# A decoder layer on one core: the sample's products with cached keys in three pinned steps

## The chip, the core and the metric

The kernel runs on one core of a Trainium2 chip. The core has five engines that run their own instruction streams: TensorE (PE, matmuls; its weight loads are listed apart as PEld), VectorE (DVE), ScalarE (ACT), GpSimd (POOL) and SyncE (SP), which here issues all transfers. [...] The metric is the time of one execution in microseconds on the device: before the change 1337.19 us, the median of three runs (1336.5 to 1340.72).

## The reference

One layer of a hybrid decoder, for a prompt of 2048 tokens and a sample of 8 batches with 8 new tokens each. After an RMS norm, one input projection gives queries, keys and values for 8 heads of 64 (mixer A), the inputs of a gated linear attention (mixer B) and two gates. Mixer A is attention over three dilated windows:

```python
DILATED = ((128, 1), (512, 4), (2048, 16))

def attend_prompt(q, k, v):
    return dilated_mixture([dilated_branch_prompt(qf, kf, vf, w, d) for w, d in DILATED])

def attend_sample(k_past, v_past, q, k, v):
    k_buf = jnp.concatenate([k_past, k], axis=1)
    v_buf = jnp.concatenate([v_past, v], axis=1)
    return dilated_mixture([dilated_branch_sample(qf, k_buf, v_buf, w, d) for w, d in DILATED])
```

For the sample, each of the 64 new tokens (batch b, step t) needs the products of its query with some of the 2048 cached keys of its batch: the last 128, every fourth of the last 512, and every sixteenth of all. What is computed here is the scores `s = einsum('bthd,btnhd->bthn', q, keys) * hd ** -0.5` for dilations 4 and 16. A token's keys for dilation 16 are its own (128 rows of stride 16 from row t); for dilation 4, tokens t and t + 4 share 128 rows.

## The kernel before, in words

**Stages.** (1) Up to about 440 us the prompt is projected to v, q and k, four tiles of 128 tokens at a time (`first(m)`, m = 0 to 3), while the attention of dilations 1 and 4 over the tiles projected earlier is fed in between (`pump`). (2) Then the projection `qkb` runs with the rest of that attention and the one of dilation 16 (`branch3`, whose queries and keys are brought by transposing loads `T_q`, `T_k`). (3) From about 740 us the projections `g`, `vb` and `gb` run beside the gated linear attention (`gla_prompt`) and its sample part. (4) From about 1090 us the output projection (`Y`, L1652) runs beside the sample's softmax and values (`sample_pair`).

**Attention of one unit** (`attend`): TensorE makes scores `s` (L444), VectorE masks and finds the maximum (`p`, L452), ScalarE takes exponentials (L455), TensorE transposes (`t`, L462), and the transposed weights are split into a high and a low half of 16 bits each (`split`). Every other split makes the low half on VectorE (L425, after ScalarE's L424), every other one on GpSimd (L429, after ScalarE's L427 and L428). Then TensorE multiplies with the values (`O`, L477), and ScalarE and VectorE bring the result out (L493, L494).

**Products with cached keys.** For a token t of batch b, `sample_keys` loads the query repeated on 128 partitions (`qb`, L981), the keys of dilation 16 (`k3`, L983) and, for t below 4, those of dilation 4 (`k2`, L986), each 128 x 512 in two buffers. `sample_scores` calls `dot` twice: GpSimd multiplies keys and query into `pr` (L965), which has one buffer, and VectorE sums each 64 of it (L970). After the eighth token a batch's 128 scores are stored (L976). `scores_of` makes a list of 49 steps of this for batches 0 to 5: step i loads token i and multiplies and sums token i - 1. Tokens are taken in the order 0, 4, 1, 5, 2, 6, 3, 7. From m = 2 one step is taken after each projected tile (24 in all), the others are woven into the `qkb` stage (`dots`). For batches 6 and 7, in stage 3, a loop of its own (`late_dots`) does it in three steps, with four buffers of `pr` and products at L1509, and with each step's instructions queued behind the last decay (L236) on GpSimd and the last `qbd` (L252) on VectorE.

**What sets the order.** The program text is written in woven order, but a scheduler places each engine's instructions: among those whose inputs and buffers it holds to be ready by its own estimate of time, the one written first. So an instruction whose inputs are there early can come to stand ahead of others that were written before it. `tc.issue_after(ins)` keeps all instructions of its block that run on the engine of `ins` behind `ins`; it makes no wait on the chip, it only fixes a place in the engine's order. Each engine runs its list strictly in that order, SyncE's transfers too, so one that waits holds all behind it.

## Time and profile before

| what | value |
|---|---|
| median of the runs (three) | 1337.19 us |
| the profiled execution | 1341.12 us, span from first to last instruction 1339.3 us |
| granted TensorE clock, mean | 0.977 |
| busy: PE, PEld | 1215.7 us (91%), 726.8 us (54%) |
| busy: DVE, ACT, POOL | 924.8 us (69%), 876.6 us (65%), 635.4 us (47%) |
| transfers | 285.27 MB, mean 213 GB/s |

In the lines of the profile, `L965 POOL TENSOR_TENSOR pr<-k,qb x96` is line 965 of the kernel before, on GpSimd, with output and inputs by the program's names and the count. "Idle before, releaser" is time in which an engine stood before an instruction, and the instruction or transfer that ended it. A busy TensorE is one with a matmul in its pipeline; that pipeline isn't always at its peak.

### The profile page before, as it was taken

How to read it: one execution, taken by the hardware profiler on the slowest of the kernel's cores; microseconds unless marked ns; L12 is line 12 of the kernel's file. 1: busy time of each engine (PE TensorE's matmuls, PEld its weight loads, DVE VectorE, ACT ScalarE, POOL GpSimd, SP SyncE). 2: the span in 40 equal slices, each digit the busy share in tenths (PEclk: the TensorE clock that was granted, in tenths of full speed). 3: DMA queues.
4: the chain of work that ended last, by engine and by line, in shares of the span. 5: the costliest groups of instructions: out<-in, count | busy, mean ns of one | idle time of the engine just before them, and what ended most of it. 6: DMA issues, size and time to landing. Idle time of an engine off the chain costs nothing.

```text
span 1339.3 us, 26206 instructions
## 1 busy us (share of the span) xinstructions
PE 1215.7 (91%) x8878; PEld 726.8 (54%) x8878; DVE 924.8 (69%) x2275; ACT 876.6 (65%) x2332; POOL 635.4 (47%) x598
## 2 busy tenths in 40 slices
PE   3798999888899798998989899999999979999998
PEld 1343565555566555576667566676554434444443
DVE  6367767788677966776755988777682288778751
ACT  5655787777568875878986666666773366554630
POOL 0076554778678735661113975666362133232220
PEclk9998999999999999999999999999999989999999
DMA  8859856767966599969986556553236679998952
GB/s 256 248 159 254 234 174 155 208 204 216 222 180 192 174 265 281 317 208 212 214 186 184 171 179 200 163 156 119 88 126 192 193 229 342 358 380 293 320 191 79
DMA packets 251800, 285.27 MB, mean 213 GB/s; under 512 B 125441, under 2 KB 160338, under 8 KB 251666
## 3 DMA queue, kind: packets, MB, share of 16 engines
q1 hardware_dynamic: 251666, 283.60, 70.9%
q8 instruction: 70, 1.15, 0.4%
q14 instruction: 64, 0.52, 0.1%
HBM read 183.12 MB, written 75.24 MB: 193 GB/s over the span
## 4 chain that ended last, share of the span: by engine, by line
PE 38%; DVE 18%; DMA 16%; POOL 9%; issue 9%; ACT 8%; SPq 2%; POOLq 0%; DVEq 0%; ACTq 0%
PE Y L1652 4%; PE acc_qkb L1127 3%; PE acc_vb L1127 3%; PE acc_v L1127 3%; PE acc_g L1127 3%; PE acc_gb L1127 3%; PE O L477 3%; PE t L462 3%; PE s L444 3%; DVE qbd L252 3%; PE acc_q L1127 2%; DMA T_q<-qp_d 2%; POOL pr L965 2%; PE acc_k L1127 2%; DMA sv<-in_cache_v_win 2%
## 5 line engine op out<-in xcount | busy, mean ns | idle before, releaser
L1127 PEld LDWEIGHTS <-hr 128*128 128x128 f16 x1824 | 174.5, 99 | 134.3 <-issue 17.4
L1127 PEld LDWEIGHTS <-hl 128*128 128x128 f16 x1248 | 122.1, 100 | 151.8 <-issue 24.3
L455 ACT ACTIVATE p<-p,o 128x256 f32<-128x256 f32 (+1 forms) x384 | 173.3, 456 | 46.4 <-DVE o L452 39.4
L1652 PE MATMUL Y<-w_o,mh 128*128 128x512 f16 x768 | 176.7, 381 | 1.8 <-ACT mh L1611 1.8
L965 POOL TENSOR_TENSOR pr<-k,qb 128x512 f32<-128x512 f32 x96 | 132.5, 1381 | 91.2 <-DVE sck L970 57.1
L429 POOL TENSOR_TENSOR pt<-p,pt 128x512 f16<-128x512 f32 (+1 forms) x80 | 94.2, 1178 | 158.4 <-ACT pt L428 142.6
L477 PE MATMUL O<-v,pt 128*128 128x128 f16 x1200 | 111.4, 222 | 25.5 <-POOL pt L429 9.2
L1652 PEld LDWEIGHTS <-mh 128*128 128x128 f16 x768 | 72.0, 98 | 88.6 <-issue 6.3
L970 DVE TENSOR_REDUCE sck<-pr 128x8 f32<-128x512 f32 x128 | 85.6, 678 | 49.0 <-POOL pr L965 48.8
L462 PE MATMUL t<-ident,p 128*128 128x128 f32 x600 | 107.5, 284 | 8.1 <-ACT p L455 3.5
L1694 POOL TENSOR_TENSOR tc<-oc,w 128x512 f32<-128x512 f32 x32 | 45.2, 1432 | 141.9 <-DVE w L1686 119.1
L477 PEld LDWEIGHTS <-pt 128*128 128x128 f16 x1200 | 82.5, 99 | 51.2 <-POOL pt L429 14.1
L1127 PE MATMUL acc_v<-w_v,hl 128*128 128x512 f16 x384 | 96.4, 396 | 8.1 <-DMA hl<-early_ht 4.0
L1127 PE MATMUL acc_g<-w_g,hr 128*128 128x272 f16 (+1 forms) x768 | 102.6, 279 | 0.0
L452 DVE CUSTOM_DVE_ANT_0 p<-s,m3w,scl_s 128x128 f32<-128x128 f32 (+1 forms) x256 | 88.9, 394 | 11.6 <-PE s L444 6.2
L1127 PE MATMUL acc_q<-w_q,hl 128*128 128x512 f16 x384 | 91.6, 387 | 3.5 <-ACT zs_k L677 2.2
L244 ACT ACTIVATE E<-D_e 128x256 f32<-128x256 f32 x168 | 66.3, 417 | 43.5 <-POOL D_e L236 25.6
L1127 PE MATMUL acc_vb<-w_vb,hr 128*128 128x512 f16 x384 | 92.3, 389 | 2.4 <-ACT zg L733 2.4
L1127 PE MATMUL acc_k<-w_k,hl 128*128 128x512 f16 x384 | 89.9, 379 | 3.4 <-ACT zs_k L677 3.0
L444 PE MATMUL s<-kk,qq 128*128 128x256 f16 (+1 forms) x512 | 82.4, 272 | 9.7 <-DMA kk<-kp_d 6.1
L1127 PE MATMUL acc_gb<-w_gb,hr 128*128 128x512 f16 x384 | 87.1, 380 | 0.0
L462 PEld LDWEIGHTS t<-ident,p 128*128 128x128 f32 x600 | 69.4, 145 | 18.1 <-ACT p L455 8.1
(510 smaller groups left out, 2637.4 us busy)
## 6 DMA issues: line engine op xcount, KB each, us to landing
k<-in_cache_k_win SPq DMA_DIRECT2D x104, 256.0 KB
sv<-in_cache_v_win SPq DMA_DIRECT2D x24, 1024.0 KB
hr<-h_d SPq DMA_DIRECT2D x44, 512.0 KB
qb<-q_d SPq DMA_DIRECT2D x64, 256.0 KB
o_d<-o SPq DMA_DIRECT2D x96, 132.0 KB
oc<-o_d SPq DMA_DIRECT2D x48, 264.0 KB
x<-in_x_prompt SPq DMA_DIRECT2D x16, 512.0 KB
h_d<-hl SPq DMA_DIRECT2D x16, 512.0 KB
```

Of the source, the lines that this page charges most:

```text
L244: ACT.activation(ev[rows, i], dv[rows, :, half, :], AF.Exp, scale=(2 * half - 1) / 16.0)
L429: POOL.tensor_tensor(l, f, h, ALU.subtract)
L444: PE.matmul(s_ps[:, i * w : (i + 1) * w], q, k, start=(n == 0), stop=(n == len(prods) - 1),)
L452: DVE.tensor_tensor_reduce(s[:, sl], s_ps[:, sl], mask, neg, BIG, ALU.add, ALU.min, nmf(i))
L455: ACT.activation(s[:, sl], s[:, sl], AF.Exp, bias=nmf(i), scale=-1.0, accum_out=denf(i))
L462: PE.transpose(p_ps[:, i * P : (i + 1) * P], t["s"][:, i * P : (i + 1) * P], ident[:])
L477: PE.matmul(o_, t["pt"][:, c, (i * nb + b) * P : (i * nb + b + 1) * P], vf(i, b), start=(n == 0), stop=(n == 2 * nb - 1),)
L965: POOL.tensor_tensor(pr[:], kt, qt, ALU.mult)
L970: DVE.tensor_reduce(out, pr[:].rearrange("p (u k d) -> p u k d", u=2, k=4), AX.X, ALU.add)
L1127: PE.matmul(z, a_[:, k, :], w[:, p_, k, cols], start=(k == 0 and i == 0), stop=(k == KT - 1 and i == 2),)
L1652: PE.matmul(Y[:], a_[:, k, :], w_[:, part, k, :512], start=(i == 0), stop=(i == len(prods) - 1),)
L1694: eng.tensor_tensor(t_[:], oc[:, g, :, 0:64], w[:, g].unsqueeze(2).to_broadcast([P, NH, HD]), ALU.mult,)
```

## The change

`scores_of` now has 50 steps and works in three: step i loads token i, multiplies token i - 1 (`products`) and sums token i - 2. Products are written over the keys, except those of `k2` for t below 4, which are needed again for token t + 4 and go to `pr`. The key tile of dilation 16 gets a third buffer. Each step's instructions are placed behind the latest split's low half on GpSimd and on VectorE (`pins`). Batches 6 and 7 use the same code, with the pins at decay and `qbd` as before. The temporary `t1` of the q and k stage is taken from another pool, one that is given back after that stage. The number of products, sums and loads stays.

```diff
--- before.py
+++ after.py
@@ -253,7 +253,8 @@
                 qbd[:, :, :n].rearrange("p i (m B) -> p i m B", B=B),
                 qv[:, :, 1, :].unsqueeze(1).to_broadcast([P, 2, M, B]), ev[:, 1:3], ALU.mult,
             )
-            st["pins"] = (dec.ins, que.ins)
+            pins["POOL"], pins["DVE"] = dec.ins, que.ins
+            gla_on.append(li)
 
         def back(self, li):
             st, n, C, nch, B = self.st, self.n, self.C, self.nch, self.levels[li]
@@ -422,11 +423,13 @@
             h, l = out
             if split_[0] % 2:
                 ACT.activation(h, in_, AF.Copy, scale=P_SCALE)
-                DVE.scalar_tensor_tensor(l, in_, P_SCALE, h, ALU.mult, ALU.subtract)
+                pins["DVE"] = DVE.scalar_tensor_tensor(
+                    l, in_, P_SCALE, h, ALU.mult, ALU.subtract
+                ).ins
             else:
                 ACT.activation(f, in_, AF.Copy, scale=P_SCALE)
                 ACT.activation(h, f, AF.Copy)
-                POOL.tensor_tensor(l, f, h, ALU.subtract)
+                pins["POOL"] = POOL.tensor_tensor(l, f, h, ALU.subtract).ins
 
         def attend(tag, nh, nb, scores, mask, vf, nmf, denf, OT, pre=None, post=None, neg=-1.0):
 
@@ -694,7 +697,7 @@
                 ct[:n, :, :g], cs[:n].unsqueeze(2).to_broadcast([n, 2, g, 64]),
                 tabs[:n, :, i0 : i0 + g], ALU.mult,
             )
-            t1 = zp.tile([P, 2, 512], F32, name=f"t1_{tag}", tag="z3", bufs=1)
+            t1 = xp.tile([P, 2, 512], F32, name=f"t1_{tag}", tag="z3", bufs=1)
             t2 = zp.tile([P, 2, 512], F32, name=f"t2_{tag}", tag="z4", bufs=1)
             z4 = zs[:n, :g].rearrange("p g (h two d) -> p g h two d", two=2, d=32)
             t24 = t2[:n, :g].rearrange("p g (h two d) -> p g h two d", two=2, d=32)
@@ -959,12 +962,6 @@
         q_s = q_d[S : S + NS, :]
         sk_state = {"pool": sk}
 
-        def dot(out, kt, qt, tag):
-            sk = sk_state["pool"]
-            pr = sk.tile([P, 512], F32, name=f"pr_{tag}", tag="pr", bufs=1)
-            POOL.tensor_tensor(pr[:], kt, qt, ALU.mult)
-            sum_of(out, pr)
-
         def sum_of(out, pr):
 
             DVE.tensor_reduce(
@@ -979,35 +976,45 @@
             sk = sk_state["pool"]
             qt = sk_state["q", t] = sk.tile([P, 512], F32, name=f"qb_{b}_{t}", tag="qbc")
             SP.dma_start(qt[:], q_s[8 * b + t : 8 * b + t + 1, :].to_broadcast([P, 512]))
-            k3 = sk_state["k3", t] = sk.tile([P, 512], F32, name=f"k3_{b}_{t}", tag="k3")
+            k3 = sk_state["k3", t] = sk.tile([P, 512], F32, name=f"k3_{b}_{t}", tag="k3", bufs=3)
             SP.dma_start(k3[:], ck[b].rearrange("(m r) c -> r m c", r=16)[t])
             if t < 4:
                 k2 = sk_state["k2", t] = sk.tile([P, 512], F32, name=f"k2_{b}_{t}", tag="k2")
                 SP.dma_start(k2[:], ck[b, W - 512 : W, :].rearrange("(j r) c -> r j c", r=4)[t])
 
-        def sample_scores(b, t):
-            if t == 0:
-                sk_state["sc"] = sk_state["pool"].tile(
-                    [P, 2, 64], F32, name=f"sck_{b}", tag="sc"
-                )
-            sc = sk_state["sc"]
-            out = sc[:].rearrange("p g (u t k) -> p g t u k", u=2, t=8)[:, :, t]
-            qt = sk_state["q", t]
-            dot(out[:, 1], sk_state["k3", t][:], qt[:], f"3_{b}_{t}")
-            dot(out[:, 0], sk_state["k2", t % 4][:], qt[:], f"2_{b}_{t}")
-            if t == 7:
-                keep_scores(b, sc)
+        pins = {}
 
         def scores_of(batches):
             todo = [(b, t) for b in batches for t in (0, 4, 1, 5, 2, 6, 3, 7)]
+            scs, sums = [], []
+
+            def products(b, t):
+                sk = sk_state["pool"]
+                if t == 0:
+                    scs.append(sk.tile([P, 2, 64], F32, name=f"sck_{b}", tag="sc"))
+                out = scs[-1][:].rearrange("p g (u t k) -> p g t u k", u=2, t=8)[:, :, t]
+                for g, k_ in ((1, sk_state["k3", t]), (0, sk_state["k2", t % 4])):
+                    pr = k_
+                    if g == 0 and t < 4:
+                        pr = sk.tile([P, 512], F32, name=f"pr_{b}_{t}", tag="pr", bufs=1)
+                    POOL.tensor_tensor(pr[:], k_[:], sk_state["q", t][:], ALU.mult)
+                    sums.append((out[:, g], pr))
 
             def step(i):
-                if i < len(todo):
-                    sample_keys(*todo[i])
-                if i:
-                    sample_scores(*todo[i - 1])
-
-            return [lambda i=i: step(i) for i in range(len(todo) + 1)]
+                with ExitStack() as order:
+                    for p_ in pins.values():
+                        order.enter_context(tc.issue_after(p_))
+                    for out, pr in sums:
+                        sum_of(out, pr)
+                    sums.clear()
+                    if i > 1 and todo[i - 2][1] == 7:
+                        keep_scores(todo[i - 2][0], scs.pop(0))
+                    if i < len(todo):
+                        sample_keys(*todo[i])
+                    if 0 < i <= len(todo):
+                        products(*todo[i - 1])
+
+            return [lambda i=i: step(i) for i in range(len(todo) + 2)]
 
         nwa = kp.tile([P, KT], F32, name="nwa")
         ACT.activation(nwa[:], nw[:], AF.Abs)
@@ -1255,7 +1262,7 @@
         full = gst.tile([P, 8, P], F32, name="full")
         POOL.memset(full[:], 0.0)
 
-        mixed = set()
+        mixed, gla_on = set(), []
 
         ob_ss = kp.tile([P, 4 * (NT + 1)], F32, name="ob_ss")
         POOL.memset(ob_ss[:], 1.0)
@@ -1476,38 +1483,13 @@
         def late_dots():
             for _ in range(6):
                 yield
-            scs = []
             sk_state["pool"] = c_sk.enter_context(
                 tc.tile_pool(name="sk3", bufs=2, reuse_waits="tile")
             )
-            todo = [(b, t) for b in range(6, 8) for t in (0, 4, 1, 5, 2, 6, 3, 7)]
-            prods, sums = [], []
-            for i in range(len(todo) + 2):
-                while "pins" not in st:
-                    yield WAIT
-                with ExitStack() as order:
-                    for p_ in st["pins"]:
-                        order.enter_context(tc.issue_after(p_))
-                    for out, pr in sums:
-                        sum_of(out, pr)
-                    if i > 1 and todo[i - 2][1] == 7:
-                        keep_scores(todo[i - 2][0], scs.pop(0))
-                    if i < len(todo):
-                        sample_keys(*todo[i])
-                    sums = []
-                    if 0 < i <= len(todo):
-                        b, t = todo[i - 1]
-                        if t == 0:
-                            scs.append(sk_state["pool"].tile(
-                                [P, 2, 64], F32, name=f"sck_{b}", tag="sc"
-                            ))
-                        out = scs[-1][:].rearrange("p g (u t k) -> p g t u k", u=2, t=8)[:, :, t]
-                        for g, k_ in ((1, sk_state["k3", t]), (0, sk_state["k2", t % 4])):
-                            pr = sk_state["pool"].tile(
-                                [P, 512], F32, name=f"pr{g}_{b}_{t}", tag="pr", bufs=4
-                            )
-                            POOL.tensor_tensor(pr[:], k_[:], sk_state["q", t][:], ALU.mult)
-                            sums.append((out[:, g], pr))
+            while not gla_on:
+                yield WAIT
+            for f in scores_of(range(6, 8)):
+                f()
                 yield
             c_sk.close()
             mixed.add("dots")
```

In the order of GpSimd, first quarter of the m = 2 stage, batch 0's tokens 5, 2, 6, 3 (a `pr` in the first, `k` or `pr` in the second, is the output of a product; `pt` is a low half, `t_qk`, `ra_qk`, `qr_qk`, `rv_qk`, `ct_qk` belong to the norm and rotation of q and k). Before:

```order
L429 TENSOR_TENSOR pt_1_0_2_1_3071<-p_1_0_2_1_2930,pt_1_0_2_1_3071 128x512
L135 TENSOR_SCALAR ra_qk_3400<-ra_qk_3400 128x16
L136 TENSOR_TENSOR qr_qk_3397<-ra_qk_3400,rr_qk_3399 128x16
L965 TENSOR_TENSOR pr_0_2_3438<-k_0_2_3293,qb_2_3291 128x512
L429 TENSOR_TENSOR pt_1_0_3_1_3160<-p_1_0_3_1_3079,pt_1_0_3_1_3160 128x512
L965 TENSOR_TENSOR pr_0_2_3441<-k_0_2_3295,qb_2_3291 128x512
L965 TENSOR_TENSOR pr_0_6_3570<-k_0_6_3436,qb_6_3434 128x512
L429 TENSOR_TENSOR pt_1_0_0_1_3258<-p_1_0_0_1_3165,pt_1_0_0_1_3258 128x512
L965 TENSOR_TENSOR pr_0_6_3573<-k_0_2_3295,qb_6_3434 128x512
L965 TENSOR_TENSOR pr_0_3_3693<-k_0_3_3566,qb_3_3564 128x512
L965 TENSOR_TENSOR pr_0_3_3696<-k_0_3_3568,qb_3_3564 128x512
```

And now:

```order
L432 TENSOR_TENSOR pt_1_0_0_1_3252<-p_1_0_0_1_3160,pt_1_0_0_1_3252 128x512
L1000 TENSOR_TENSOR k_0_5_3167<-k_0_5_3167,qb_5_3165 128x512
L1000 TENSOR_TENSOR k_0_1_3028<-k_0_1_3028,qb_5_3165 128x512
L432 TENSOR_TENSOR pt_1_0_1_1_3350<-p_1_0_1_1_3257,pt_1_0_1_1_3350 128x512
L1000 TENSOR_TENSOR k_0_2_3289<-k_0_2_3289,qb_2_3287 128x512
L1000 TENSOR_TENSOR pr_2_3433<-k_0_2_3291,qb_2_3287 128x512
L704 TENSOR_TENSOR t_qk_3796<-zs_q_3659,ct_qk_3794 128x1024
L710 TENSOR_TENSOR t_qk_3797<-zs_q_3659,ct_qk_3794 128x16x32 x2
L122 TENSOR_SCALAR rv_qk_3784<-qs_q_3660 128x16
L432 TENSOR_TENSOR pt_1_0_2_1_3494<-p_1_0_2_1_3358,pt_1_0_2_1_3494 128x512
L1000 TENSOR_TENSOR k_0_6_3430<-k_0_6_3430,qb_6_3428 128x512
L1000 TENSOR_TENSOR k_0_2_3291<-k_0_2_3291,qb_6_3428 128x512
```

Each pair of products now stands behind a low half (L429, now L432), with the next one behind the pair; before, products stood singly or in threes between other work.

In the order of VectorE about the same place, the sums (L970, now L967). Before:

```order
L970 TENSOR_REDUCE sck_2885<-pr_0_5_3300 128x2x4
L425 SCALAR_TENSOR_TENSOR pt_1_0_3_0_3111<-t_1_0_3_0_3106,pt_1_0_3_0_3111 128x512
L713 TENSOR_TENSOR t_qk_3411<-t_qk_3410,qr_qk_3397 128x1024
L759 SCALAR_TENSOR_TENSOR vp_3554<-acc_v_3463,vp_3554 128x8x64
L452 ISA p_1_0_0_1_3165,o_1_0_0_3093<-s_1_0_0_1_3164,m3w,scl_s 128x256
L452 ISA o_1_0_0_3093 128x1
```

And now:

```order
L542 SCALAR_TENSOR_TENSOR ht_3840<-x_2547,rs_3830,ht_3840 128x1024
L426 SCALAR_TENSOR_TENSOR pt_1_0_3_0_3536<-t_1_0_3_0_3531,pt_1_0_3_0_3536 128x512
L967 TENSOR_REDUCE sck_2885<-k_0_2_3289 128x2x4
L967 TENSOR_REDUCE sck_2885<-pr_2_3433 128x2x4
L455 ISA p_1_1_0_1_3601,o_1_1_0_3518<-s_1_1_0_1_3600,m3c,scl_s 128x256
L455 ISA o_1_1_0_3518 128x1
```

The two sums of a token now stand side by side behind a split (L425, now L426), later than the split after which their products stand on GpSimd; before, each stood by itself where its product was estimated to end.

In the order of SyncE, at the third `T_q` of the dilation 16 branch. Before:

```order
L874 DMA o_d<-o_3_1_0_7261 128x264
L155 DMA zqk_e_9831<-zqk_d 128x2x512
L155 DMA zqk_e_10052<-zqk_d 128x2x512
L976 DMA sc_d<-sck_7617 128x128
L874 DMA o_d<-o_3_1_1_7354 128x264
L909 DMA_TRANSPOSE T_q_7756<-qp_d 128x8x128
L909 DMA_TRANSPOSE T_k_7758<-kp_d 128x8x128
L874 DMA o_d<-o_3_1_2_7452 128x264
L730 DMA zqk_d<-zq_8451 128x512
L567 DMA hr_8483<-h_d 128x2048
L909 DMA_TRANSPOSE T_q_7870<-qp_d 128x8x128
```

And now:

```order
L912 DMA_TRANSPOSE T_q_7691<-qp_d 128x8x128
L912 DMA_TRANSPOSE T_k_7693<-kp_d 128x8x128
L877 DMA o_d<-o_3_1_2_7392 128x264
L980 DMA k_5_2_7828<-in_cache_k_win 128x512
L983 DMA k_5_2_7830<-in_cache_k_win 128x512
L570 DMA hr_9462<-h_d 128x2048
L733 DMA zqk_d<-zq_8765 128x512
L978 DMA qb_2_7826<-q_d 128x512
L912 DMA_TRANSPOSE T_q_7804<-qp_d 128x8x128
L912 DMA_TRANSPOSE T_k_7806<-kp_d 128x8x128
L877 DMA o_d<-o_3_1_3_7486 128x264
L980 DMA k_5_6_7941<-in_cache_k_win 128x512
```

Before, all loads of keys and queries for batches 0 to 5 stand ahead of this place. Now those of the last tokens of batch 5 stand among the transposing loads.

## The prediction

> **What bounds the kernel now.** First the stretches of the span. Columns after the length: busy us (instructions) of TensorE matmuls, weight loads, VectorE, ScalarE, GpSimd, then granted TensorE clock, DMA share, GB/s.
>
> ```profile
> 120.00:240.00 120.00, 116.89 (x778) 67.36 (x777) 81.79 (x224) 89.04 (x262) 59.04 (x68) 0.99 0.74 195
> ...
> 240.00:480.00 240.00, 210.76 (x1506) 133.81 (x1505) 193.06 (x473) 178.32 (x499) 181.88 (x162) 0.97 0.74 208
> 480.00:600.00 120.00, 113.10 (x847) 73.45 (x845) 81.43 (x228) 90.62 (x258) 67.28 (x54) 0.99 0.91 260
> ...
> 600.00:740.00 140.00, 128.25 (x1162) 97.19 (x1160) 88.62 (x367) 113.72 (x403) 28.86 (x29) 0.95 0.82 201
> 740.00:930.00 190.00, 180.20 (x1614) 124.60 (x1613) 156.08 (x231) 120.50 (x325) 133.09 (x108) 0.98 0.52 163
> ...
> 1080.00:1100.00 20.00, 10.80 (x57) 5.60 (x56) 16.57 (x40) 11.96 (x21) 12.06 (x10) 0.74 0.66 196
> ```
>
> TensorE sets the pace nearly everywhere, so time can only be won where it stands still. From 120 to 240 us, with projections and prompt attention but no cached keys, it is idle 3.1 of 120 us (2.6%). From 240 to 480, the same two kinds of work with the products over cached keys woven in, it is idle 240 - 210.76 = 29.2 us (12%). From 480 to 600 it is 6.9 us, with DMA at 0.91. GpSimd goes from 49% busy to 76%.
>
> Next, who waits for whom around the products: what the product's engine and the sum's engine sat idle for (us, times).
>
> ```profile
> L965 POOL TENSOR_TENSOR pr<-k,qb x96: 1261/1272/2259, 240.5 to 595.5; 128x512 f32<-128x512 f32 x96
> ...
>   DVE sck L970: 57.1, 42
> ...
> L970 DVE TENSOR_REDUCE sck<-pr x128: 666/678/687, 241.8 to 925.1; 128x8 f32<-128x512 f32 x128
> ...
>   POOL pr L965: 48.8, 38
> ```
>
> GpSimd stood 57.1 us before a product because the one buffer `pr` still waited for its sum on VectorE; VectorE stood 48.8 us before a sum because its product wasn't done. The two engines hold each other in turn, and all that is queued behind is held too. Third, what this does to TensorE between 240 and 600 us (us in total, times, longest), with three waits of the chain in front of it:
>
> ```profile
> PE O L477 <- POOL pt L429: 8.3, 12, 1.4
> PE s L444 <- DMA kk<-kp_d: 6.1, 2, 4.6
> PE t L462 <- ACT p L455: 3.5, 5, 1.5
> PE s L444 <- DVE o L452: 3.5, 5, 2.2
> PE O L477 <- DMA v<-vp_d: 3.3, 2, 2.0
> PE O L477 <- ACT pt L428: 2.9, 2, 2.3
> PE O L477 <- DVE o L494: 2.3, 1, 2.3
> ...
> ACT p L455 <- DVE o L452: 33.7, 25, 4.5
> POOL pt L429 <- ACT pt L428: 22.2, 17, 5.6
> ```
>
> The largest is the value product (L477) waiting for the low half of the weights, which GpSimd makes (L429), the instruction that stands between products. VectorE's masks (L452) are late for ScalarE's exponentials (33.7 us, 25 times), and through L455, L452 and L494 for TensorE (9.3 us). One instance in order of time, first GpSimd, then VectorE:
>
> ```profile
> 378.11 2.19 POOL L965 TENSOR_TENSOR pr<-k,qb 128x512 f32<-128x512 f32 x1 [3.42 <-DVE sck L970]
> 381.09 1.27 POOL L965 TENSOR_TENSOR pr<-k,qb 128x512 f32<-128x512 f32 x1 [0.80 <-DVE sck L970]
> 382.77 1.17 POOL L429 TENSOR_TENSOR pt<-p,pt 128x512 f16<-128x512 f32 x1 [0.41 <-ACT pt L428]
> ...
> 375.92 1.39 DVE L818 COPY qq<-qq 64x2048 f16<-64x2048 f16 x2 [2.45 <-DMA qq<-qp_d]
> 377.35 0.69 DVE L970 TENSOR_REDUCE sck<-pr 128x8 f32<-128x512 f32 x1
> 377.95 1.22 DVE L713 TENSOR_TENSOR t_qk<-t_qk,qr_qk 128x1024 f32<-128x1024 f32 x1
> ```
>
> The sum stood on VectorE behind a copy that waited 2.45 us for a transfer; GpSimd waited 3.42 us for that sum. A late transfer for one attention block thus became a stop of an engine that had nothing to do with it.
>
> **The change part by part.** The sum: profiled execution 1341.12 us (span 1339.3 and 1.8 around it), which is 3.9 above the median 1337.19 of the runs. I work out a difference and apply it to the median.
>
> *(a) Sums a step behind their products, products in place, both pinned behind the latest split.* Same instructions: 96 products of 1.38 us on average and 96 sums of 0.68 us, none added. Their order moves. A product no longer needs the sum ahead of it, since its result lies in the key tile, or in a `pr` that was read a step before; by the order shown above the prediction a sum stands some two splits behind its product. The pins do not make an engine wait at run time; they keep a product from standing ahead of an earlier split. Upper end: the stretch 240 to 480 falls to the idle share of 120 to 240, 0.026 x 240 = 6.2 us, so 29.2 - 6.2 = 23.0 us are won. Lower end: nothing. In between lies the list of waits. What the mutual stop can account for is L429's 8.3 us and the 9.3 us behind VectorE, 17.6 in all; the rest is late transfers and ScalarE. L429 also waited 22.2 us for ScalarE, as in the last GpSimd row above, and that stays. I take 60% of 23.0, which is 13.8, near three quarters of the 17.6. From 480 to 600 the excess is 6.9 - 3.1 = 3.8 us, but DMA is nearly full there: I take 1.
>
> *(b) The third key buffer.* A key tile is now held through its sum, so loads would come a step later with two buffers. SyncE's own waits from 240 to 600 us:
>
> ```profile
> SPq L983 <- POOL pr L965: 33.0, 18, 5.2
> SPq L981 <- POOL pr L965: 27.2, 23, 4.4
> ```
>
> SyncE stood 60.2 us before loads of keys and queries whose buffer a product held, with transposes of `kk` and `qq` and loads of `v` queued behind. With GpSimd freed, these buffers come free sooner; the k3 loads have a spare one. The two-buffer k2 tiles and the queries have none. This is how the 9.4 us of TensorE waiting for `kk` and `v` could shrink; it is inside (a)'s upper end, and I add nothing. The query loads' wait does not depend on the sums.
>
> *(c) Two steps more of delay, one step more in number.* The last products move past the end of dilation 4's attention. GpSimd's order has no product behind the last L429 of that branch before, and 12 now; with them go 12 sums and the loads of some 5 steps, about 12 transfers of 256 KB, 3 MB. They fall into the stretch from 600 us, which is bound by other loads:
>
> ```profile
> DVE T_q L818 <- DMA T_q<-qp_d: 26.6, 11, 3.4
> ```
>
> The work of 12 x 1.38 = 16.6 us on GpSimd (busy 28.86 of 140) and 12 x 0.68 = 8.2 us on VectorE (88.62 of 140) has cover. If it stood uncovered on VectorE it would cost 8.2 us. The transfers have little: 3 MB at 201 GB/s is 15 us of DMA time at a share of 0.82, but the same bytes leave the stretch before. Between 0 and 8 us, I take 3, since only some of those loads stand directly ahead of a `T_q`.
>
> *(d) Batches 6 and 7, 740 to 930 us.* Already in three steps and pinned; what changes is in-place products instead of four `pr` buffers. SyncE's waits there:
>
> ```profile
> SPq L983 <- POOL pr L1509: 14.4, 10, 3.0
> ...
> SPq L981 <- POOL pr L1509: 7.5, 10, 1.3
> ```
>
> Smaller than before by far, with DMA at 0.52. A key tile is held for a sum longer, and k3 has a tile more: 0, between -2 and +2.
>
> *(e) The tile t1 in another pool.* No instruction changes, but the room that later pools get does. In the last stage the sample's memsets and first loads stand earlier, ahead of TensorE's first output transposes:
>
> ```profile
> 1092.30 1.04 PE L1610 MATMUL tm<-ident,mt 128*128 128x128 f16 x8 [8.86 <-ACT mt L1600]
> ...
> 1088.22 0.42 SPq L1762 DMA_DIRECT2D hm<-in_c_hm  x1
> ...
> 1092.02 0.45 SPq L1778 DMA_DIRECT2D ls_q<-q_d  x1
> ```
>
> TensorE stands 8.86 us there. Sample transposes (L1781, L1807, L1830) can fill up to some 3 us of that if their loads land in time; if these land late, the first transpose of the output waits behind them. Between -3 and +3; I take -1, because the loads now stand ahead of three `oc` loads.
>
> Sum: -13.8 - 1 + 0 + 3 + 0 - 1 = -12.8 us, so 1324.4; I say 1325. All lower ends: -23.0 - 3.8 - 2 - 3 = -31.8, 1305. All upper ends: +8 + 2 + 3 = +13, 1350.
>
> [...] Products have a minimum of 1.261 us, but a mean of 1.381:
>
> ```profile
> L965 POOL TENSOR_TENSOR pr<-k,qb 128x512 f32<-128x512 f32 x96 | 132.5, 1381 | 91.2 <-DVE sck L970 57.1 <-DMA qb<-q_d 9.9 <-PE O L477 6.3
> ```
>
> The one at 378.11 took 2.19 us while VectorE ran L713 until 379.17; 379.17 + 1.27 is 380.44, its end was 380.30. So it ran after L713, not beside it. [...] Excess so far: 96 x (1.381 - 1.272) = 10.5 us. [...]
>
> **The rivals.** A measurement of this kernel tells a change from none at about 0.3%, 4 us.
>
> *More is won.* TensorE's idle share falls all the way to that of 120 to 240, `kk` and `v` come in time too: -23 - 2 + 3 - 1 = -23, 1314. For it: the 60.2 us of SyncE's waits; against: DMA at 0.74 is no less in 120 to 240, but the 22.2 us that GpSimd waits for ScalarE stay.
>
> [...]
>
> *Another wait takes the place.* TensorE's next limits are ScalarE (22.2 us for L428) and transfers. If L429 comes no earlier because ScalarE or the step's two back-to-back products (2.8 us) hold it, only some 5 us are won and 3 given back: 1335, no change.
>
> *Slower: the loads of late steps among those of dilation 16.* SyncE issues in order. Between the `T_q` transposes now stand some 12 loads of keys and queries, each of which can wait for a buffer that a pinned product or sum on a busy engine holds. At the mean of the waits above, 60.2/41 = 1.5 us, they hold the queue 18 us, in a stretch where `T_q` is already what is late (26.6 us). If two thirds of that reach TensorE, 12 us, and (a) yields 6: 1337.2 + 6 = 1343. It decides once (a) yields less than what the held `T_q` cost. Against: GpSimd is only 21% busy there, so buffers come free at once.
>
> **How the numbers follow.** The forecast (1318 to 1331) 0.41; more won 0.18; ports 0.10; another wait 0.17; slower 0.14. Forecast and more won are faster by over 0.3%, and so are two thirds of the ports' case: 0.66. Same: 0.17 + 0.03 = 0.20. Slower: 0.14. The likeliest's own range is 1318 to 1331; to leave out 2 in 10, half of the slower case and the far end of more won, the range is 1309 to 1341.
>
> **What would show it.** Right: GpSimd's idle time before products put down to L970 nearly gone (from 57.1), VectorE's before sums under 10 (from 48.8); TensorE idle between 240 and 480 us near 15 instead of 29; its wait for L429 below 4 us; the end of the dilation 4 branch some 13 us earlier. (c) right: products after 600 us with TensorE's idle share from there to the end of dilation 16 little changed. [...] Wrong altogether: TensorE's idle time as before with ScalarE or DMA as what ended it, or the gain up to 600 us gone by 740.

## The result, and the profile after

The changed kernel takes 1346.03 us (median of four runs, 1345.03 to 1346.35). Beside it the kernel before took 1337.19 us (median of three runs of 1336.5 to 1340.72; a fourth, disturbed one of 2480 us is left out). The ratio is 1.0058, 95% interval 1.0035 to 1.0080: **slower** by 0.6%, where 1325 us had been predicted with a range up to 1341. The same two kernels run again (e13 below) give 1.0053 (1.0035 to 1.0071). The profiled execution of the changed kernel took 1345.03 us (span 1343.2, mean granted clock 0.973).

To see where the time went, TensorE's own work serves as a ruler, since both kernels have the same matmuls. The view of a source line gives for each kind of matmul the count, the duration in ns (min/median/max), and when the first and the last of them started. Kernel before: projections of k, the last three quarters of qkb, gb; scores of dilation 16; output products.

```profile
L1127 PE MATMUL acc_k<-w_k,hl x384: 376/379/379, 83.8 to 441.7; 128*128 128x512 f16 x192
L1127 PE MATMUL acc_gb<-w_gb,hr x384: 379/379/390, 954.5 to 1083.1; 128*128 128x512 f16 x192
L1127 PE MATMUL acc_qkb<-w_qkb,hr x288: 379/379/631, 501.3 to 617.9; 128*128 128x512 f16 x144
...
L1652 PE MATMUL Y<-w_o,mh x768: 379/379/634, 1094.5 to 1334.5; 128*128 128x512 f16 x192
...
L444 PE MATMUL s<-T_k,T_q x256: 216/219/314, 599.5 to 713.2; 128*128 128x128 f16 x128
```

The same view of the changed kernel:

```profile
L1134 PE MATMUL acc_k<-w_k,hl x384: 377/380/380, 88.1 to 432.2; 128*128 128x512 f16 x192
L1134 PE MATMUL acc_gb<-w_gb,hr x384: 378/380/391, 954.8 to 1081.5; 128*128 128x512 f16 x192
L1134 PE MATMUL acc_qkb<-w_qkb,hr x288: 378/380/391, 489.5 to 597.4; 128*128 128x512 f16 x144
...
L1634 PE MATMUL Y<-w_o,mh x768: 378/380/635, 1097.9 to 1338.4; 128*128 128x512 f16 x192
...
L447 PE MATMUL s<-T_k,T_q x256: 216/220/315, 591.1 to 712.6; 128*128 128x128 f16 x128
```

From these rows, in us:

| stretch | before | after | difference | predicted |
|---|---|---|---|---|
| A: start to first k product | 83.8 | 88.1 | +4.3 | 0 (b) |
| B: first to last k product | 357.9 | 344.1 | -13.8 | -13.8 (a) |
| C: to the first score of dilation 16 | 157.8 | 158.9 | +1.1 | -1 (a) |
| D: first to last score of dilation 16 | 113.7 | 121.5 | +7.8 | +3 (c) |
| E: to the last gb product | 369.9 | 368.9 | -1.0 | 0 (d) |
| F: to the first output product | 11.4 | 16.4 | +5.0 | -1 (e) |
| G: output products | 240.0 | 240.5 | +0.5 | |

The sum is +3.9, the difference of the two spans. The profiled execution of before lay 3.9 above its median and that of after 1.0 below, so the spans differ by 4.9 less than the medians, and the table tells where time went, but not all of the slowdown. B came out as forecast, and three others took it back and more: A, D and F, +17.1 together.

**The mutual stop is gone.** Groups of GpSimd's and VectorE's instructions in the changed kernel (busy us, mean ns | idle us just before, and what ended it):

```profile
L1000 POOL TENSOR_TENSOR k<-k,qb 128x512 f32<-128x512 f32 x96 | 135.8, 1429 | 13.0 <-DMA qb<-q_d 13.0
L1000 POOL TENSOR_TENSOR pr<-k,qb 128x512 f32<-128x512 f32 x32 | 43.3, 1354 | 0.4 <-DVE sck L967 0.4
...
L967 DVE TENSOR_REDUCE sck<-k 128x8 f32<-128x512 f32 x96 | 62.9, 675 | 0.4 <-POOL k L1000 0.3
L967 DVE TENSOR_REDUCE sck<-pr 128x8 f32<-128x512 f32 x32 | 21.6, 674 | 0.4 <-POOL pr L1000 0.4
```

GpSimd waits 0.4 us for sums (57.1 before), VectorE 0.7 us for products (48.8 before). TensorE's busy time by stretches (columns as in the prediction):

```profile
240.00:480.00 240.00, 220.60 (x1609) 142.54 (x1606) 191.67 (x476) 190.78 (x534) 175.93 (x159) 0.97 0.74 206
480.00:600.00 120.00, 117.63 (x885) 76.25 (x884) 75.51 (x230) 86.77 (x251) 59.20 (x48) 1.00 0.89 265
600.00:740.00 140.00, 118.68 (x1050) 90.61 (x1048) 94.07 (x361) 106.90 (x379) 40.98 (x38) 0.93 0.80 201
```

TensorE's idle time falls from 29.2 to 19.4 us and from 6.9 to 2.4, 14.4 in all, against 14.8 forecast. From 600 to 740 us it rises from 11.75 to 21.3.

**Where the last 600 to 740 us differ.** The first 40 us of that stretch, before:

```profile
600.00:640.00 40.00, 35.38 (x338) 27.63 (x336) 27.30 (x132) 33.96 (x126) 5.79 (x5) 0.91 0.86 210
```

and after:

```profile
600.00:640.00 40.00, 28.51 (x245) 24.16 (x243) 32.55 (x123) 30.14 (x109) 18.78 (x15) 0.74 0.95 214
```

TensorE is busy 6.9 us less, at a lower granted clock (0.74 against 0.91). Counted in the trace, the first score of dilation 16 stands behind 335 of the 384 qkb products before the change and behind 366 after it: the rows above show it too, since that score precedes the last qkb product by 18.4 us before and by 6.3 us after. Eleven of these products in a row, in the order of time of the kernel before:

```profile
586.61 2.54 PE L1127 MATMUL acc_qkb<-w_qkb,hr 128*128 128x512 f16 x11
```

With 0.38 us for the last one, that is (2.54 - 0.38) / 10 = 0.216 us from one to the next, and 31 of them are 6.7 us. TensorE did them earlier, in its former idle time, and then had them no more to fill its pauses in dilation 16. Beside dilation 16, 13 products now run on GpSimd, none before. Their key loads show in SyncE's list. Transposing loads of one residue before, and then after, where two key loads went out some 2 us ahead of them:

```profile
602.31 1.28 SPq L909 DMA_TRANSPOSE T_q<-qp_d  x1
603.64 1.29 SPq L909 DMA_TRANSPOSE T_k<-kp_d  x1
```

```profile
602.20 2.36 SPq L912 DMA_TRANSPOSE T_q<-qp_d  x1
604.61 2.86 SPq L912 DMA_TRANSPOSE T_k<-kp_d  x1
```

On VectorE after the change, the copy of `T_q` stood waiting for its transfer, with a result of the attention (L497) behind it, for which TensorE stood 4.53 us, until 612.10:

```profile
610.10 0.85 DVE L821 COPY T_q<-T_q 64x1024 f16<-64x1024 f16 x2 [4.26 <-DMA T_q<-qp_d]
...
611.53 0.42 DVE L497 TENSOR_TENSOR o<-O,ol 128x256 f32<-128x256 f32 x1
```

Summed over the 32 transposing loads, the hold on the queue grew from 48.3 to 57.4 us, but VectorE's waits for `T_q` fell to 16.7 us in all (26.6 before), so late `T_q` alone doesn't explain the stretch. C and D together are 8.9 us longer: 5.6 us of that is more idle time of TensorE (32.7 in place of 27.1) and 3.3 us more busy time, at a lower clock (0.97 and 0.92, before 0.98 and 0.94) and with fewer matmuls.

**The early start.** SyncE's list in order of time, before:

```profile
24.39 0.42 SPq L983 DMA_DIRECT2D k<-in_cache_k_win  x1
...
31.98 6.69 SPq L542 DMA_TRANSPOSE hl<-early_ht  x2
```

and after:

```profile
24.66 0.90 SPq L980 DMA_DIRECT2D k<-in_cache_k_win  x2
...
33.15 8.23 SPq L545 DMA_TRANSPOSE hl<-early_ht  x2
```

With a third key buffer the scheduler lets one more key load of 256 KB go out ahead of the transposing loads of the first activations. Two of these hold the queue 8.23 us in place of 6.69, and TensorE waits 5.7 us in all for them before products of v, 4.0 before the change:

```profile
PE acc_v L1134 <- DMA hl<-early_ht: 5.7, 2, 4.8
```

**The last stage.** TensorE in order of time, with its idle time and what ended it, after:

```profile
1089.53 0.69 PE L1763 MATMUL ts_q<-ident,ls_q 64*128 64x64 f32 x4 [7.65 <-DMA ls_q<-q_d]
1092.96 0.66 PE L1763 MATMUL ts_k<-ident,ls_k 64*128 64x64 f32 x4 [2.13 <-DMA ls_k<-k_d]
1097.94 1.89 PE L1634 MATMUL Y<-w_o,mh 128*128 128x512 f16 x4 [0.27 <-ACT mh L1593]
```

The sample's transposes (L1763, L1781 before) now stand ahead of the output's and wait for two loads in turn. Before, the output's transposes came first (1092.30, shown in the prediction), and output products began 11.4 us behind the last gb product, not 16.4.

### The profile page after: what moved, and what is told of

Same layout as the page of the kernel before. It is cut to its first block, busy times and chain, and to the rows that moved or that the text cites. A ratio compares the mean times of both kernels' runs of the same rounds, so it can differ in the third digit from the quotient of the medians.

```text
span 1343.2 us, 26225 instructions
## 1 busy us (share of the span) xinstructions
PE 1218.8 (91%) x8878; PEld 731.2 (54%) x8878; DVE 929.4 (69%) x2275; ACT 876.5 (65%) x2332; POOL 633.6 (47%) x598
## 4 chain that ended last, share of the span: by engine, by line
PE 40%; DVE 19%; DMA 12%; issue 10%; ACT 9%; POOL 7%; SPq 2%; DVEq 0%; POOLq 0%; ACTq 0%
PE acc_qkb L1134 5%; PE Y L1634 4%; PE acc_gb L1134 3%; DVE qbd L252 3%; PE acc_q L1134 3%; PE acc_vb L1134 3%; PE acc_g L1134 3%; PE O L480 3%; PE acc_v L1134 3%; PE s L447 3%; DMA T_q<-qp_d 3%; PE acc_k L1134 3%; PE t L465 2%; DVE p L455 1%; DVE sck L967 1%
## 5 line engine op out<-in xcount | busy, mean ns | idle before, releaser
L1134 PEld LDWEIGHTS <-hl 128*128 128x128 f16 x1248 | 122.2, 100 | 151.1 <-issue 27.8
L432 POOL TENSOR_TENSOR pt<-p,pt 128x512 f16<-128x512 f32 (+1 forms) x80 | 93.9, 1174 | 228.1 <-ACT pt L431 191.4
L1000 POOL TENSOR_TENSOR k<-k,qb 128x512 f32<-128x512 f32 x96 | 135.8, 1429 | 13.0 <-DMA qb<-q_d 13.0
L1134 PE MATMUL acc_k<-w_k,hl 128*128 128x512 f16 x384 | 93.1, 379 | 2.0 <-ACT zs_k L680 1.6
L447 PE MATMUL s<-kk,qq 128*128 128x256 f16 (+1 forms) x512 | 79.1, 267 | 1.8 <-DVE o L455 1.8
L236 POOL TENSOR_TENSOR D_e<-b_e 128x512 f32<-128x512 f32 x56 | 68.7, 1240 | 15.7 <-DVE b_e L223 9.7
```

The costliest lines, as they stand in the source:

```text
L236: dec = POOL.tensor_tensor(dv, bv, bv[:, :, 0:1, B - 1 : B].to_broadcast([P, M, 2, B]), ALU.subtract)
L432: pins["POOL"] = POOL.tensor_tensor(l, f, h, ALU.subtract).ins
L447: PE.matmul(s_ps[:, i * w : (i + 1) * w], q, k, start=(n == 0), stop=(n == len(prods) - 1),)
L1000: POOL.tensor_tensor(pr[:], k_[:], sk_state["q", t][:], ALU.mult)
L1134: PE.matmul(z, a_[:, k, :], w[:, p_, k, cols], start=(k == 0 and i == 0), stop=(k == KT - 1 and i == 2),)
```

## The experiments

All ratios are to runs of the kernel before made beside them, with 95% intervals; 0.1% is 1.3 us. The columns A to F are the stretches above, from one profiled execution each; two profiles of the changed kernel differ by up to 1.7 us in a stretch, but A runs from 82.7 to 86.1 in kernels whose early loads stand alike, and single runs of a kernel scatter with a standard deviation of some 3 us. So a difference of 3 us in one stretch of one row is no more than noise. "Beside D": products that ran on GpSimd during D. "Two and old" means two key buffers, and t1 in its old pool.

| run | kernel | ratio | A | B | C | D | E | F | beside D |
|---|---|---|---|---|---|---|---|---|---|
| | before | 1 | 83.8 | 357.9 | 157.8 | 113.7 | 369.9 | 11.4 | 0 |
| e13 | after, again | 1.0053 (1.0035-1.0071) | 88.1 | 345.8 | 159.4 | 122.6 | 368.4 | 16.3 | 13 |
| e14 | after, two buffers | 1.0025 (1.0008-1.0041) | 82.7 | 341.7 | 159.9 | 122.4 | 369.8 | 15.2 | 13 |
| e2 | after, two and old | 0.9988 (0.9971-1.0005) | 83.3 | 340.8 | 160.6 | 122.8 | 369.1 | 10.7 | 13 |
| e3 | before, t1 moved | 1.0039 (1.0019-1.0059) | 83.7 | 356.4 | 160.4 | 110.3 | 368.2 | 17.2 | 0 |
| e12 | e2 without pins | 1.0187 (1.0160-1.0214) | 83.2 | 367.0 | 166.7 | 115.2 | 367.8 | 10.8 | 0 |
| e15 | before with pins | 1.0004 (0.9984-1.0023) | 84.3 | 352.7 | 158.5 | 118.2 | 371.3 | 10.1 | 15 |
| e1 | after, woven steps x1.3 | 1.0032 (1.0016-1.0048) | 85.9 | 345.2 | 165.5 | 113.3 | 368.2 | 16.7 | 2 |
| e4 | after, woven steps x2 | 1.0172 (1.0142-1.0201) | 86.2 | 343.0 | 177.8 | 120.2 | 368.8 | 15.5 | 0 |
| e6 | e2, woven steps x1.3 | 1.0024 (1.0010-1.0037) | 86.1 | 339.9 | 170.4 | 111.9 | 371.2 | 10.1 | 3 |
| e9 | e2, 4 steps a tile | 1.0068 (1.0046-1.0091) | 83.7 | 343.8 | 167.9 | 122.2 | 374.8 | 10.0 | 8 |
| e10 | e2, 5 steps a tile | 1.0127 (1.0101-1.0153) | 86.0 | 357.1 | 166.0 | 114.3 | 372.7 | 10.3 | 1 |
| e16 | e2, batch 5 later | 1.0057 (1.0041-1.0073) | 85.6 | 342.0 | 152.9 | 116.9 | 384.8 | 10.0 | 7 |
| e5 | e2, g and vb sooner | 0.9982 (0.9966-0.9999) | 84.2 | 341.2 | 167.6 | 117.3 | 366.1 | 10.9 | 14 |
| e7 | before, g and vb sooner | 1.0024 (1.0006-1.0042) | 83.8 | 356.1 | 168.1 | 101.6 | 368.1 | 10.0 | 0 |
| e8 | e6 and e5 | 1.0077 (1.0048-1.0107) | 84.1 | 342.3 | 171.9 | 116.4 | 372.9 | 10.2 | 4 |
| e11 | e14, third buffer for T_q | 1.0062 (1.0039-1.0086) | 85.1 | 341.3 | 165.2 | 118.4 | 371.4 | 16.7 | 13 |

### Undoing the third buffer and t1's place: e2, e3, e13, e14

```diff
-            k3 = ... tag="k3", bufs=3)      # e2, e14
+            k3 = ... tag="k3")
-            t1 = xp.tile(... tag="z3", bufs=1)      # e2; e3: the kernel before with xp
+            t1 = zp.tile(... tag="z3", bufs=1)
```

> The changed kernel with two key buffers of dilation 16 again, and t1 in its old pool; three steps, in place and pins stay. If the third buffer costs the 3 us by which the first projections are late at 120 to 220 us (it lets one more 256 KB key load go out among the loads of weights), and t1's place the 2 to 4 us of the last stage, both vanish: some 1340 us. If both come from the order of the steps, the time stays at 1345 to 1347. If two buffers make the key loads wait for the sums a step later, the stretch 240 to 480 us loses up to 5 us of its gain: up to 1351.

> The kernel before with nothing changed but the pool of t1. If the last stage's 2 to 4 us come from the room that t1's place gives to or takes from the pools behind it, the time is 1341 to 1343 us with TensorE's idle time grown only from 1090 us on; if not, it is that of before, 1337 to 1340.

> The changed kernel itself, beside the three that follow and the same runs of the kernel before: 1344 to 1347 us if the first comparison holds.

> The changed kernel with two key buffers of dilation 16, t1 in its new pool. With both undone it took 1335 us, and t1's move alone cost the kernel before 5.3 us. If the third buffer has a price of its own (the early key load among the first weights' loads, 4 us), this one takes 1339 to 1342; if the whole difference is t1's, 1344 to 1347; if two buffers hold the loads back, over 1347.

From e13 to e14, the third buffer costs 1.0053 - 1.0025 = 0.28%, 3.7 us (1.4 to 6.1 by the scatter of the runs); A falls from 88.1 to 82.7, and the queue is as before. In e14's list for SyncE:

```profile
32.05 6.37 SPq L545 DMA_TRANSPOSE hl<-early_ht  x2
```

and TensorE's wait for them there is 1.1 us. With a third buffer the queue is held 8.23 (after) and 8.27 us (e13) there, with two 6.69 (before) and 6.37 us (e14); in the table A is 85.9 to 88.1 us with a third buffer (after, e13, e1, e4) and 82.7 to 86.1 with two.

t1's place costs 0.39%, 5.2 us, in the kernel before (e3), and 1.0025 - 0.9988, 4.9 us, between e14 and e2. In e3 nothing else was changed, and its TensorE shows the same order as the changed kernel:

```profile
1087.45 0.68 PE L1781 MATMUL ts_q<-ident,ls_q 64*128 64x64 f32 x4 [8.11 <-DMA ls_q<-q_d]
1091.63 0.65 PE L1781 MATMUL ts_k<-ident,ls_k 64*128 64x64 f32 x4 [2.88 <-DMA ls_k<-k_d]
1096.23 1.27 PE L1652 MATMUL Y<-w_o,mh 128*128 128x512 f16 x4
```

In every kernel of the table with t1 in the new pool F is 15.2 to 17.2 us, in every one with the old pool 10.0 to 11.4. Both terms are shown, and within noise they add: without them the change is worth -0.12% (-0.29 to +0.05), no measurable change. What is left to explain is why three pinned steps, which win 12 to 17 us in B, win nothing by the end.

### Pins and steps, one without the other: e12, e15

```diff
-                    for p_ in pins.values():      # e12: batches 0 to 5 without pins
+                    for p_ in pins.values() if todo[0][0] > 5 else ():
-                if i < len(todo):      # e15: the kernel before, its step inside the pins
-                    sample_keys(*todo[i])
+                with ExitStack() as order:
+                    for p_ in pins.values():
+                        order.enter_context(tc.issue_after(p_))
+                    if i < len(todo):
+                        sample_keys(*todo[i])
...
```

> The kernel with two key buffers and t1 back, with the pins of batches 0 to 5 left out: three steps and products in place stay, and the scheduler places them where it holds their inputs to be ready. It then puts nearly all key loads ahead of 440 us. Theory D: as with 40 steps there, or better, 1322 to 1330, and the pins are what keeps the loads late. Theory F: products and sums stand ahead of the splits of their time, TensorE's wait for the low half of the weights rises again over 8 us from 240 to 480, and the time is 1337 to 1346.

> The kernel before, with its product and sum of one step left as they are, but each step pinned behind the latest split on GpSimd and VectorE. Leaving the pins out of the kernel with two buffers and t1 back cost it 26 us. If the pins alone do the good, 1325 to 1334; if they only serve sums that stand a step behind (a pinned sum right behind its product waits 1.3 us or more for it, and the next product for the sum), 1340 to 1355.

Without pins the scheduler puts the loads and products early: 78 of the 96 products run ahead of the last k product (42 in the changed kernel, 51 before). B is 367.0, 9 us worse than before, and the splits are late. TensorE's wait from 240 to 480 us in e12:

```profile
PE O L480 <- POOL pt L432: 13.9, 13, 3.4
```

With pins on the old two steps the mutual stop stays. GpSimd's and VectorE's waits in e15, same stretch:

```profile
POOL pr L968 <- DVE sck L973: 24.8, 20, 3.2
...
DVE sck L973 <- POOL pr L968: 15.7, 16, 2.3
```

(31.4 and 23.7 in the kernel before.) In e12, in the same stretch, GpSimd waits 1.6 us for sums, but VectorE 30.8 for products, so without pins only one half of the stop is gone. The gain in B was had with both halves only: three steps alone lose 1.9%, pins alone do nothing. Why e12's B is so long isn't separated: the splits are late (13.9 us, 6.1 before), but e12 also runs 38 products more in B than e2 (78 and 40), and at the price found below for e10 that number alone would cost more than the 26.2 us by which its B is longer than e2's.

### Moving the late products and loads: e1, e4, e6, e9, e10

```diff
-        weave(host, att, [...], [dots(), len(side) + 3])
+        weave(host, att, [...], [dots(), 1.3 * (len(side) + 3)])      # e1, e6; e4: 2.0
...
                     yield from project(name, [t])
                     dot_next()
+                dot_next()      # e9; e10: twice
```

> The changed kernel, but the steps that are woven into the qkb stage are taken 1.3 times as often, so that all loads of cached keys stand ahead of the third transposing load T_q; nothing is left out. Theory A, the loads stand in the way: 600 to 740 us is slow in the changed kernel because key and query loads lie between the transposing loads of dilation 16; without them most of the some 20 us won by 600 us is kept at 740 us, and the time is 1346 less 10 to 18, 1328 to 1336 us. Theory B, the stage has its own pace: 16 residues at some 7 us each from a start that hardly moves; TensorE then only waits in another place, the stage ends at 740 us +-2 as in both kernels, and the time is 1343 to 1347 us.

> As the 1.3 times kernel, but the woven steps are taken twice as often: all key loads end some ten steps of qkb before the third T_q, at the price of denser products and loads from 450 to 560 us, where the transfers' share is already near 1. Theory A, the loads stand in the way: as the 1.3 times kernel or up to 4 us faster, since a queue with no backlog meets the first T_q. Theory B, the stage's own pace: 1343 to 1347 us. A third way: the denser loads take back what is won between 480 and 600 us, and this kernel is slower than the 1.3 times one by 3 to 8 us.

> The kernel with two key buffers and t1 back (1335 us), and the woven product steps taken 1.3 times as often, so that key loads end before the third transposing load; g and vb as they were. Theory A: the pace of the residues falls from 8.2 to 7.7 us and their start keeps its lead, so 1324 to 1329. Theory C: TensorE still has nothing beside dilation 16 from 600 to 640 us; only the pace's share comes back, 1329 to 1334.

> The kernel with two key buffers and t1 back (1335 us), but four product steps for each tile of 240 to 440 us in place of three, so 32 steps there and 18 in the qkb stage. Theory D, transfers bound 440 to 720 us: there the transfers' share is 0.8 to 1.1, so a key load costs about as much among qkb's projections as among the transposing loads, and only one that is moved ahead of 440 us (share 0.74) is free; eight steps are 3 MB, at 200 to 270 GB/s 11 to 15 us of transfers, of which a third to a half shows: 1328 to 1332. Theory F, GpSimd and VectorE are full before 440 us (72% and 79% busy): the eight steps cost 8 x 2 x 1.4 = 22 us of GpSimd there, late splits hold TensorE again, and the time is 1336 to 1342.

> The same with five steps for each tile: 40 steps ahead of 440 us, 10 in the qkb stage, and all key loads ended before the third transposing load. Theory D: 1322 to 1330, with the last score of dilation 16 some 10 us earlier than in the kernel with two key buffers and t1 back. Theory F: slower than with four steps, 1340 to 1350, with the first projections' end some 10 us later than there.

With at most 4 products beside it D takes 101.6 to 120.2 us, in seven of nine kernels 110 to 117; with 7 or more it takes 117 to 123. So products and loads beside dilation 16 go with a D some 6 to 8 us longer, as theory A says. The hold of the 32 transposing loads is not all of it: it is 57.4 us in the changed kernel and 45.5 in e1, but 48.8 in e9, with the longer D, and 53.1 in e6, with the shorter. But e1 and e6, which move them ahead, pay it in C: 165.5 and 170.4 in place of 158.9 and 160.6. e4 packs them twice as dense and C becomes 177.8. Moving them ahead of the last k product is no better: from e9 to e10, 14 more products in B (50 and 64) cost 13.3 us there. Theory D, that transfers alone bound 440 to 720 us, falls: in e10 only 32 of the 96 products and their loads are left behind the last k product, and C and D together take 280.3 us, as in the changed kernel (280.4). Theory F fits better: about 0.95 us a product from e9 to e10, with its sum and loads; from 240 to 480 us GpSimd and VectorE are busy 184.5 and 201.0 of 240 us in e9 (77 and 84%) and 199.2 and 202.4 in e10 (83 and 84%). From e2 to e9, though, ten products more cost only 3.0 us in B, and e9 and e10 took some 5 us more than theory F's ranges allow. e4 and e6 too came out above every range given for them, and e1 (1340.92 us) between those of A and B.

e9 answers another doubt. The changed kernel has run 42 products by the last k product and the kernel before 51, so part of B's gain could be work put off. e9 has run 50, and its B is 343.8: the gain of 14 us stands at an equal number of products. Nor was attention put off: the changed kernel ran 44 of its matmuls more in B than the kernel before.

### Moving a whole batch out: e16, e17, e18

```diff
-                side.extend(scores_of(range(6)))
+                side.extend(scores_of(range(5)))
-            for f in scores_of(range(6, 8)):
+            for f in scores_of(range(5, 8)):
-        late = [late_dots(), 25]
+        late = [late_dots(), 34]      # e17: 28, e18: 25
-        late = [[late[0], 2] for g, n in left if g is late[0]]
+        late = [[late[0], 4] for g, n in left if g is late[0]]      # e17; e18: 8
```

> The kernel with two key buffers and t1 back (1335 us), with batch 5 moved out to the later loop, which then does batches 5 to 7 between 740 and 930 us, where the transfers' share is 0.52 and GpSimd 70% busy. Nothing is left out. If the products of 440 to 640 us are what costs (their loads between the transposing loads, their sums and products beside the attention), dilation 16 ends some 6 to 10 us earlier and 1326 to 1331 is left; if the later loop pays the same for them, 1334 to 1338.

> Batch 5 in the later loop again, but the loop spread over a longer stretch (28 of the stage's steps for its 26, and the rest beside gb), so that its products stand no denser among the gated attention's decays than the two batches did. With batch 5 in the later loop dilation 16 ended 15.8 us earlier, and 15 us were given back between 790 and 870 us, where GpSimd was 82% and VectorE 91% busy. If the density is what costs there, most of the 15 us stay: 1324 to 1331. If every step costs TensorE its 0.7 us wherever it stands, or the sample's gated attention, pushed to the end, holds up the output stage: 1336 to 1344.

> As the one before, thinner still (25 of the stage's steps for 26, eight for the rest). If density is what costs: 1322 to 1329, no slower than the one before. If the sample's part at the end holds up the output stage, slower than the one before by 2 to 6 us.

With 16 products gone from C and D, the lead at the last k product (14 us in e16) is kept, and grows to 16 at the last score. Scores of dilation 16 in e16:

```profile
L447 PE MATMUL s<-T_k,T_q x256: 216/219/314, 580.5 to 697.4; 128*128 128x128 f16 x128
```

and in e2, with the batch in its place:

```profile
L447 PE MATMUL s<-T_k,T_q x256: 216/219/314, 584.7 to 707.5; 128*128 128x128 f16 x128
```

C and D together take 269.8 us in place of 283.4: 13.6 us for 16 products. But E takes 384.8 in place of 369.1, 15.7 more (it is 366 to 375 in all kernels with two batches there, however late dilation 16 ended): the later loop pays about the same price. The time, 1345.54 us, is above both ranges named. TensorE from 740 to 840 us in e16, then in e2:

```profile
740.00:840.00 100.00, 81.54 (x694) 57.09 (x694) 92.53 (x129) 60.21 (x157) 80.42 (x63) 0.93 0.59 180
```

```profile
740.00:840.00 100.00, 92.54 (x809) 63.36 (x809) 90.00 (x133) 64.98 (x170) 74.89 (x60) 0.97 0.55 169
```

e17 and e18, which were to thin that loop out, missed for another reason (ratios 1.0249 and 1.0227): the sample's gated attention waits for the loop to end, slid behind the last gb product, and F became 70.7 and 62.2 us. Whether a thinner loop is cheaper stays open.

### Filling dilation 16, or speeding it: e5, e7, e8, e11

```diff
-        weave(host, att, [chain(load_w("g"), load_w("vb")), 4 * KT], [dots(), ...])
+        weave(host, att, [chain(load_w("g"), load_w("vb")), 6 * KT], [dots(), ...])      # e5, e7 (kernel before), e8 (and x1.3 as e6)
-                t = b3.tile([P, nb, P], F16, ..., tag=f"T{nm_}")
+                t = b3.tile([P, nb, P], F16, ..., tag=f"T{nm_}", bufs={"q": 3, "k": 2}[nm_])      # e11
```

> The kernel with two key buffers and t1 back (1335 us), and the weights of g and vb prepared sooner: their loads and scaling are woven into the qkb stage 1.5 times as often, so that projections of vb and g stand on TensorE from the fourth residue of dilation 16 on, not from the eighth. Nothing is left out, and the key loads still lie between the transposing loads. Theory C, no work to fill with: dilation 16 has its own pace of some 8 us a residue, and after the change TensorE has no projections beside it from 600 to 640 us, because qkb ended some 20 us earlier while g and vb start where they did; with g and vb sooner TensorE's idle time from 600 to 660 us falls from some 17 us to under 7 and the time is 1322 to 1329. Theory A, the loads between the transposing loads: these are as many as before, so 1333 to 1337.

> The kernel before with the weights of g and vb prepared 1.5 times as soon, nothing else. Here qkb's projections last until the fourth residue and TensorE is idle 11.8 us of 600 to 740, most of it from 620 to 640. Theory C: there is less to fill than after the change, so the gain is smaller: 2 to 6 us, 1330 to 1334. If it gains as much as the changed kernel does, the filling is a thing of its own and no sign of where the change's gain went. If it gains nothing, 1335 to 1339, then the sooner loads cost in 480 to 600 us what they bring behind it.

> Both at once: key loads ended before the third transposing load, and weights of g and vb 1.5 times as soon, with two key buffers and t1 back. If A and C each hold a share, the two gains add: 1318 to 1325. If all is C, as the kernel with the weights alone, 1322 to 1329. If the denser loads from 450 to 590 us (transfers' share already near 1 there) cost more than they bring, slower than the better of the two alone.

> The changed kernel with two key buffers, t1 in its new pool (which the last stage pays with some 5 us), and the room of the third key buffer given to a third buffer of T_q. Theory E, the transposing load waits for its buffer: 5 us of a residue's 7 to 8 are its transfer, which can't start before the scores of the residue before last; with a third buffer it starts a residue sooner, residues 0 to 6 take under 6.5 us each instead of 7.1, and the last score of dilation 16 comes 5 to 10 us earlier; about 1333 with t1's price in it. Theory D, transfers are the bound: it lands no sooner, and the time is 1340 to 1343.

Theory C falls as a way to get the time back. In e5 vb's first product starts at 631.4 us in place of 649.6 in e2, but its last one at 936.1, no sooner than e2's 936.3: work that TensorE does ahead during dilation 16 didn't bring the end nearer. That what follows waits for the end of that attention is a reading of this, not shown. C grows by what D gains, in e5 (167.6 and 117.3) as in e7 (168.1 and 101.6). e5, with 0.18% (0.01 to 0.34) less than before, is the best of all kernels run, and that is less than what a reader should call a gain. A third buffer for T_q shortens D to 118.4 but lengthens C to 165.2: 1.0062 against 1.0025 without it.

## Why the prediction was wrong

**(a), right in mechanism and near in size where it was costed, wrong in what it was worth.** The stop vanished, TensorE's idle time fell by 14.4 us (14.8 forecast), B by the 13.8 taken. That the figures meet is partly luck: 240 to 480 us gave 9.8 in place of 13.8 and 480 to 600 us 4.5 in place of 1; B's 13.8 is 9.9 us less idle time and 3.9 us less busy time, which the prediction didn't count; and e13, the same kernel, has 12.1. Of the named signs, the waits went to 0.4 and 0.7 us; TensorE is idle 19.4 from 240 to 480 where 15 was named; its wait for the splits fell from 8.3 to 5.4, not below 4, since GpSimd now waits for ScalarE there:

```profile
POOL pt L432 <- ACT pt L431: 90.4, 25, 10.3
```

against 22.2 before. The step that failed is the one that applied "a difference" to the median: saved idle time of TensorE was taken for time at the end. Behind the last k product TensorE's lead didn't last to the end: the lead of 9.5 us at the last k product (17.6 in e2) was 8.4 (14.8) at the first score of dilation 16 and 0.6 (5.7) at the last one. (The profile of before took 3.9 us more than its median, so these leads look too long: the spans of e2 and before are 7.5 us apart, the means of their runs 1.2.) TensorE had put 31 qkb products ahead, 6.7 us, and was idle in dilation 16 instead.

**(b) 0, measured +3.7 alone.** The prediction looked at waits from 240 us on and not at what a free buffer lets go out at 25 us, ahead of the loads that the first matmuls wait for.

**(c) +3, measured +7.8 in D.** The place was right (13 products and their loads beside dilation 16), and its upper bound of 8 holds. "The same bytes leave the stretch before" is where it went wrong: an empty place upstream brought nothing back, C is no shorter with four products fewer (and 31 qkb products more). Its +3 went by "only some of those loads stand directly ahead of a `T_q`"; the transposing loads behind them hold the queue 9.1 us longer in all, though how much of D that makes isn't shown. Nor was it two steps of delay that moved the products there, since the edit puts only the sums one step later: with pins and the old steps (e15) 15 products run beside dilation 16, with three steps and no pins (e12) none. The runs that moved products found 13.6 us for 16 of them taken out of C and D, 15.7 for putting them into E and 13.3 for 14 more in B. That is no price for each product left, though: e10 has 32 left behind the last k product and e12 18, in place of 54 and 56, and C and D together take 280.3 and 281.9 us there, as in the changed kernel.

**(d) 0**, measured -1.0, within noise.

**(e) -1, measured +5.2 alone.** The mechanism was named, with its condition ("if these land late, the first transpose of the output waits behind them"). The condition held: 7.65 and 2.13 us of waiting for `ls_q` and `ls_k`. The +3 at its upper end has no working in the prediction; two loads waited for in turn, with the output's own transposes behind them, took more.

**The rivals.** *Ports*, in the chances with 0.10 and with two thirds of it in the 0.66 for faster: no run shows ports or turns at them, and the case was the author's estimate. What the runs showed in its place is how long the products took: those of batches 0 to 5 1.386 us on average, 1.381 before, so their excess over the median, 10.5 us for 96 of them, didn't grow (10.5 again, the median being 1.277); the in-place ones of all batches took 1.429 us. *Another wait takes the place* (1335) has the time of the three steps and pins by themselves (e2, 1335.02), but by luck: it reasoned from a gain of some 5 us, and e2's B gained 17.1. *Slower*, 1343, had the right stretch and the right loads, but reasoned from waits for buffers and a small yield of (a); what the rows show is a longer hold of the transposing loads, and it came out slower although (a) yielded all. The sentence "or the gain up to 600 us gone by 740" was the sign of a wrong forecast that came true. Sum of the five measured terms -13.8 + 1.1 + 4.3 + 7.8 + 5.0, less 0.5 for the rest, is +3.9.

So the step that failed is known, and with it 8.9 us of side costs, undone one by one; what ate the rest of the lead is not. What stays open: why C and D together take 279 to 298 us in all kernels with three steps and six batches ahead, where the kernel before takes 271.5 and e3 270.7, also with no more products left for them (45 before; 46 in e9 with 290.1 us, 32 in e10 with 280.3, 18 in e12 with 281.9). Only e16, with a batch fewer, comes below, 269.8.
